# Hybrid attention/RG-LRU block with an MLP in three-pass split floats: order of casts, evacuations and low parts in the MLP, and the side of SBUF on which the output projection's pools lie

## The chip, the cores and the metric

The kernel runs on one core of a Trainium2 chip. The metric is the device time of one execution in microseconds (us). Three runs of the kernel before took 1237.33, 1234.93 and 1236.98 us (median 1236.98); a further, profiled execution took 1230.48 us. Engine names are those of the profile: PE (matmul), DVE (VectorE), ACT (ScalarE), POOL (GpSimd), SP (the engine on whose queue nearly all DMAs are issued).

## The reference

One transformer-like layer on 1024 tokens of width 1024: a normalised input goes to stick-breaking attention (8 heads) and a gated linear recurrence, their outputs together go through `w_out` and are added to `x`; then a squared-ReLU MLP (width 4096) is added.

```python
def reference(x, ...):
    h = rms_norm(x, norm1_g[l])
    x = x + hybrid_mixer(h, w_in[l], ..., w_out[l])     # concatenate([attn, lru], -1) @ w_out
    h = rms_norm(x, norm2_g[l])
    x = x + sq_relu_mlp(h, w_up[l], w_down[l])          # jnp.square(relu(h @ w_up)) @ w_down
    return x
```

## The kernel before

**Split floats.** Each operand of a large matmul is split in two parts: a *cast* on ACT rounds it to the PE's fast 32-bit format (the high part), and a subtraction on DVE or POOL makes the *low part* (value minus high part). A product is then three matmuls: low by high, high by low, high by high. In the MLP `split2` (cast on ACT, low part on DVE) makes both, `mmc` issues the three.

**Mixer.** Attention, the recurrence's gates and their projections run interleaved; their results go to `mix_d` in DRAM. Attention's score tiles, `vv`, `qT`, `kH`, `kL` of the odd head pairs and its work pool `ap` lie on the right side of SBUF; the weights of the projections (`wp`) and the even pairs' tiles (`qkvE`) lie on the left.

**Output projection.** For two halves of 512 output columns (n = 0, 1) and eight token tiles it multiplies `mix0`/`mix1` (high and low parts of `mix_d`, loaded through raw buffers `mr`) by `wo` (from `wr_o`). `raws` (raw buffers), `wf` (the split weights of n = 0) and `ra` lie on the right side, so on tiles that attention uses to its end; `mix`, `wn0` to `wn2` and `junk` lie on the left. Its results are added to `x1`, transposed into `h2` (PE, then ACT) and squared for the second norm (ACT into `junk`).

**MLP.** The products follow two groups of 16 of the 32 feature blocks, in a seven-product scheme with two levels. A group has 112 products of 12 matmuls (128x512): up products first (first sixteen, `a` and `b`, into tiles named `p1`; then triples with the movings `t2`, `b22`, `t3`; then pairs with `t1` and `t4`), then down products in four stages (`da`/`db`, `ea`/`eb`, `ga`/`gc`, `ha`). In a product one split operand is the *stationary* (`st`, `sb`, `sda`, ...) and one the *moving* (`m0t`, `m1t`, `mda`, ...). The list `PR` holds all 224 products; the loop at the end issues, for step q, the matmuls of product q (`pr.mm`), its bank evacuation (`pr.ev`), additional work hung on that step (`pr.after`: differences of `h2` and splits of new movings), a sum of `U` tiles eight products ahead (`usum`), the stationary of product q+6 (`stat`), the moving of product q+4 (`moving`), and loads of weights as raw buffers come free. From the fifth product on the scheduler keeps this written order on each engine (`keep_in_program_order`); before that it orders by its own simulation.

In the pairs `t1`/`t4` an evacuation is one or two DVE subtractions from the bank into `U`, followed on ACT by Relu and Square of those `U` tiles, and for one of three tiles by a POOL multiplication.

**Rings.** Stationaries rotate through six buffers, movings through twelve, raw weight blocks through eight (`Ring`: the first few of each in a pool that is open early, the rest in pools opened after the output projection). A tile that takes a buffer waits until the tile that had it twelve (six, eight) allocations earlier has been read. In the `ha` stage of the first group the casts of the second group's first movings (`m1b11`, `m1b21`) are hung on the steps, one on each, between the casts of `ha`'s own movings.

**Start of the MLP.** `mlp_head`, in the middle of the second half of the output projection, closes `wf` and `raws`, opens the first pools of the rings, loads the first two weight items (two blocks each) and splits the first movings and three stationaries.

Of the kernel before, what the change touches and what calls it, by code (L numbers as in the profile page):

```python
# [9 lines left out]
F32 = mybir.dt.float32  # L10
# [9 lines left out]
P = 128  # L20
S = 1024
D = 1024
# [21 lines left out]
def kernel(ctx, tc, x, norm1_g, w_in, conv_w, conv_b, w_rg, b_rg, w_ig, b_ig,  # L44
# [463 lines left out]
    wn1 = pool(tail, "wn1")  # L508
    junk = pool(tail, "junk").tile([P, D], F32, name="junk")
    wn2 = pool(tail, "wn2", bufs=2)  # L510
    mxp = pool(tail, "mix")
    mixes = [(mxp.tile([P, KC, 512], F32R, name=f"mix{g}h"), mxp.tile([P, KC, 512], F32R, name=f"mix{g}l")) for g in range(2)]
    wpools = {(0, u): wf for u in range(4)} | {(1, 0): wn0, (1, 2): wn1, (1, 3): wn2, (1, 1): wn2}

# [52 lines left out]

    rwr, stp, mvp = Ring(4, 4), Ring(3, 3), Ring(8, 4)
    rwr.pools[0] = raws
# [69 lines left out]
    def up_group(g):  # L639
        q0 = len(PR)  # L640

        def w(i, k, j):
            return w_up[k, 16 * g + 8 * i + j]
# [36 lines left out]

        its, bks = [], []
        for j in range(8):
            its.append(Item([(f"a{g}{j}", w(0, 0, j)), (f"b{g}{j}", w(0, 1, j))], lambda r: None))
            bks.append(banked(f"p1_{g}{j}"))
        ITEMS.extend(its)

        def pa_(j):
            prod(its[j], 0, "b11", bks[j], lambda: act.copy(U[:, j, 1], bks[j]()), True, False, 1)

        def pb_(j):  # L690
            prod(its[j], 1, "b21", bks[j], lambda: relu2(j, 0, bks[j]()), False, True, 1)

# [48 lines left out]
    def down_group(g):  # L741
# [17 lines left out]
        def prod(name, q, k, key, start, stop, item, r, free, ev=None, usum=None, store=None):  # L759
# [5 lines left out]
            def mv():  # L765
                pr.mv = split2(mvp, f"m{key}{g}{k}", item.raws[r])
                if store is not None:
                    act.dma_start(store, item.raws[r])

# [64 lines left out]
    def stat(n):  # L834
        nonlocal free
        if n < len(PR):
            pr = PR[n]
            pr.item.add()
            pr.stat()
            if pr.mov is None:  # L840
                free += pr.free
        load_items(n - NSTAT)

    def moving(n, q):
# [5 lines left out]
        load_items(q)  # L850

    def mlp_head():

        early.close()
        mvp.pools[0] = pool(ctx, "ma", bufs=8, side="right")
        stp.pools[0] = pool(ctx, "sa", bufs=3, side="right")
        load_items(-NSTAT)
        for u in range(4):
            mov("0b11", u, hb(0, 0, u))
        for n in range(3):  # L860
            stat(n)
        for u in range(4):
            mov("0b21", u, hb(1, 0, u))

# [6 lines left out]
    for n in range(2):  # L871
        wo = {}
        for grp in ((0, 1, 2), (3,), (4,), (5,), (6,), (7,)) if n == 0 else tuple((t,) for t in range(NT)):
# [3 lines left out]
            for u in KO:  # L877
                if u not in wo:
                    wr = raw(f"wr_o{n}{u}")
                    nc.sync.dma_start(wr, rows2(w_out, u, 512 * n))  # L880
                    wo[u] = split((nc.gpsimd, nc.vector)[(u + n) % 2], wpair(n, u), wr)
# [33 lines left out]

    for pl, nm, n in ((rwr, "rb", 4), (stp, "sb", 3), (mvp, "mb", 4)):
        pl.pools[1] = pool(ctx, nm, bufs=n)
    U = pool(ctx, "units").tile([P, 8, 4, 512], F32, name="U")
    nc.vector.tensor_scalar_mul(nrs2, rs2, -1.0)
    limit = len(ITEMS)  # L920
    load_items(-NSTAT)
    for n in range(3, NSTAT):
        stat(n)
    for q, pr in enumerate(PR):
        pinned = q >= PINNED
        pr.mm()
        pr.ev()
        for fn in pr.after:
            fn()
        if q + UAHEAD < len(PR) and PR[q + UAHEAD].usum is not None:  # L930
# [41 lines left out]
```

## Time and profile before

| | |
|---|---|
| three runs, median (lowest to highest) | 1236.98 us (1234.93 to 1237.33) |
| the profiled execution | 1230.48 us, of which 1228.7 us from first to last instruction |
| PE, DVE, ACT, POOL busy | 94%, 75%, 49%, 45% of the span |
| mixer up to its last attention matmul | to about 447 us |
| output projection, first to last matmul | 459.25 to 555.07 us |
| MLP | 555.07 to about 1225 us; the second group from 888.84 us |

Busy time of PE is that of pipelined matmuls, so it says little of the rate. The rate is read from the number of matmuls in a stretch of given length: a 128x512 matmul without a gap comes every 0.23 us at full clock. `L577` is the one line through which all MLP operations are recorded, so they are told apart by their tiles.

### The profile page before, as it was taken

The page shows a single profiled execution, that of the slowest core. Times are in us where ns is not written, and L with a number is a line of the kernel's source. Part 1 is how long each engine was busy: PE and PEld are TensorE (multiplying, and loading weights), DVE is VectorE, ACT ScalarE, POOL GpSimd, SP SyncE. Part 2 cuts the span into 40 slices and gives each one's busy share as a digit, 9 for nine tenths or more (in the row PEclk, how much of TensorE's full clock was granted, in tenths as well). Part 3 has the DMA queues.
Part 4 walks back from the last instruction along what each step waited for, and adds up shares of the span by engine and source line. Part 5 has one row for each costly group of instructions (what it writes and reads, how often), then busy time and mean ns, then how long its engine had stood idle before and what let it go on. Part 6 is the DMA issues. An engine that isn't in the chain of part 4 may idle for free.

```text
span 1228.7 us, 16111 instructions
## 1 busy us (share of the span) xinstructions
PE 1152.3 (94%) x5410; PEld 939.5 (76%) x5410; DVE 921.1 (75%) x1458; ACT 603.2 (49%) x1203; POOL 554.0 (45%) x506
## 2 busy tenths in 40 slices
PE   8998899899999949999999969999998999699998
PEld 7876787789887637888788848778886888487787
DVE  7889998999988845235767559997747665589975
ACT  7455466566566532156523554344445245544342
POOL 1366664654455733000342356853312524468632
PEclk9999899999999879999999989999999999799999
DMA  8210011401001636003333213445533332144465
GB/s 260 61 35 35 35 47 34 133 12 50 11 13 38 216 118 210 26 17 108 117 122 95 79 48 104 159 149 172 184 107 101 118 101 69 44 128 149 134 213 173
DMA packets 80787, 123.58 MB, mean 101 GB/s; under 512 B 10256, under 2 KB 28736, under 8 KB 80704
## 3 DMA queue, kind: packets, MB, share of 16 engines
q1 hardware_dynamic: 78400, 118.35, 31.5%
q10 hardware_dynamic: 2304, 4.20, 1.0%
q8 instruction: 43, 0.70, 0.3%
q14 instruction: 40, 0.33, 0.1%
HBM read 107.83 MB, written 14.68 MB: 100 GB/s over the span
## 4 chain that ended last, share of the span: by engine, by line
PE 60%; DVE 19%; issue 8%; ACT 7%; DMA 3%; POOL 2%; SPq 0%; DVEq 0%; ACTq 0%; POOLq 0%
PE p L577 18%; PE pa L577 11%; PE pb L577 4%; PE pc L577 4%; ACT U L577 3%; PE po L63 3%; PE po L64 2%; PE po L65 2%; DVE U L577 2%; PE pd L63 2%; PE pd L64 2%; PE pd L65 2%; DVE g L415 2%; PE av L435 2%; PE z L406 1%
## 5 line engine op out<-in xcount | busy, mean ns | idle before, releaser
L416 POOL TENSOR_TENSOR w<-w,g 128x128 f32<-128x128 f32 (+3 forms) x96 | 101.6, 1067 | 99.3 <-DVE g L415 44.3
L415 DVE TENSOR_TENSOR_SCAN g<-g 128x128 f32<-128x128 f32 (+3 forms) x96 | 111.6, 1173 | 5.3 <-ACT g L410 4.1
L577 POOL TENSOR_TENSOR U<-U 128x512 f32<-128x512 f32 x48 | 70.0, 1465 | 85.7 <-ACT U L577 69.4
L577 POOL TENSOR_TENSOR r_sb<-r_sb,r_sa 128x512 f32<-128x512 f32 x16 | 23.9, 1493 | 173.5 <-DMA r_sb<-in_w_up_dram 158.8
L63 PE MATMUL pd<-wh_p,hTl 128*128 128x384 f32 x256 | 91.7, 359 | 9.4 <-DVE vv L180 4.7
L577 PE MATMUL p<-m1t,st 128*128 128x512 f32 x384 | 91.6, 398 | 4.3 <-DVE U L577 4.3
L577 PE MATMUL p<-m0t,st 128*128 128x512 f32 x384 | 91.9, 398 | 2.3 <-DVE U L577 2.3
L64 PE MATMUL pd<-wl_p,hTh 128*128 128x384 f32 x256 | 90.7, 354 | 0.3 <-DVE wl_p L60 0.3
L577 DVE TENSOR_TENSOR U<-p,U 128x512 f32<-128x512 f32 x80 | 54.9, 686 | 47.0 <-PE p L577 47.0
L577 PEld LDWEIGHTS p<-m1t,st 128*128 128x128 f32 x384 | 73.1, 191 | 21.5 <-issue 4.7
L577 ACT ACTIVATE U<-U 128x512 f32<-128x512 f32 x96 | 58.9, 629 | 60.9 <-DVE U L577 59.5
L65 PE MATMUL pd<-wh_p,hTh 128*128 128x384 f32 x256 | 88.4, 345 | 0.0
L577 PEld LDWEIGHTS p<-m0t,st 128*128 128x128 f32 x384 | 73.1, 191 | 19.8 <-issue 2.7
L577 PE MATMUL p<-m1b,sb 128*128 128x512 f32 x288 | 68.1, 393 | 1.8 <-ACT U L577 1.8
L577 PE MATMUL p<-m0b,sb 128*128 128x512 f32 x288 | 68.7, 394 | 0.0
L577 PE MATMUL pa<-mda,sda 128*128 128x512 f32 x192 | 54.0, 434 | 15.6 <-ACT mda L577 12.6
L577 PEld LDWEIGHTS p<-m1b,sb 128*128 128x128 f32 x288 | 54.0, 188 | 14.5 <-ACT U L577 2.3
L577 PEld LDWEIGHTS p<-m0b,sb 128*128 128x128 f32 x288 | 53.8, 188 | 12.2
L410 ACT ACTIVATE g<-z 128x128 f32<-128x128 f32 (+3 forms) x96 | 48.1, 501 | 27.2 <-PE z L408 15.7
L577 PEld LDWEIGHTS pa<-mda,sda 128*128 128x128 f32 x192 | 40.3, 211 | 26.8 <-ACT mda L577 13.5
L63 PEld LDWEIGHTS pd<-wh_p,hTl 128*128 128x128 f32 x256 | 49.5, 194 | 13.5 <-DVE vv L180 6.2
L430 ACT CAST wth<-pw 128x512 fp32r<-128x512 f32 (+1 forms) x80 | 42.5, 548 | 34.4 <-PE pw L426 23.9
(302 smaller groups left out, 3229.9 us busy)
## 6 DMA issues: line engine op xcount, KB each, us to landing
wr_p<-in_w_in_dram SPq DMA_DIRECT2D x24, 192.0 KB, 2.6
xt<-in_x_dram SPq DMA_DIRECT2D x8, 512.0 KB, 6.8
x<-in_x_dram SPq DMA_DIRECT2D x16, 256.0 KB, 4.5
r_a<-in_w_up_dram SPq DMA_DIRECT2D x16, 256.0 KB, 2.8
r_b<-in_w_up_dram SPq DMA_DIRECT2D x16, 256.0 KB, 4.2
wr_o<-in_w_out_dram SPq DMA_DIRECT2D x8, 512.0 KB, 3.6
mr<-mix_d SPq DMA_DIRECT2D x8, 512.0 KB, 5.0
r_sa<-in_w_up_dram SPq DMA_DIRECT2D x16, 256.0 KB
```

The source lines that it names most:

```text
L63: nc.tensor.matmul(ps, al, bh, start=start, stop=False)
L64: nc.tensor.matmul(ps, ah, bl, start=False, stop=False)
L65: nc.tensor.matmul(ps, ah, bh, start=False, stop=stop)
L406: nc.tensor.matmul(z, qT[hs, h, qr], kL[hs, k0:k0 + kn], start=False, stop=not diag)
L410: nc.scalar.activation(g[:, :kn], z, AF.Sigmoid, scale=-1.0)
L415: nc.vector.tensor_tensor_scan(gr, gr, gr, g[:, kn:kn + 1], op0=ALU.mult, op1=ALU.bypass)
L416: nc.gpsimd.tensor_tensor(w[:, :kn], w[:, :kn], g[:, 1:kn + 1], op=ALU.mult)
L430: nc.scalar.copy(wth[:, :nw], pw[:, :nw])
L435: nc.tensor.matmul(av[:, q0:256], vv[:, 2 * m + jj, h, :], wt[:, 256 * jj:256 * jj + 256 - q0], start=m == 0 and jj == 0 and wt is wtl, st ...
L577: ins = getattr(self.eng, op)(*args, **kw)
```

## The change

Three things change.

1. In the MLP's loop the order within a step becomes: matmuls, casts of the stationary (q+6) and of the moving (q+4), evacuation, low parts of these casts, the work hung on the step, the low parts of that work, loads, `usum`. `split2` issues only the cast and puts the low part on a list that `low()` issues. The store of a summed weight block (`r2`) goes to that list too.
2. The second group's first movings are cast in the last four steps of `ha`, two on each, after all of `ha`'s own movings.
3. The output projection's raw buffers and first weights lie on the left, its `mix` tiles and other weights on the right; the raw buffers are four instead of three; the rings' early and late parts are 2+6 raw, 4+2 stationaries, 8+4 movings (before 4+4, 3+3, 8+4). The first up weights are loaded as items of one block instead of two, and the MLP's early loads are issued after the output projection's last weight load.

```diff
-    raws = pool(ctx, "ra", bufs=4, side="right")
+    raws = pool(ctx, "ra", bufs=2)
     early = ExitStack()
-    wf = pool(early, "wf", bufs=4, side="right")
-    rwp = pool(early, "raws", bufs=3, side="right")
+    rwp = pool(early, "raws", bufs=4)
+    wf = pool(early, "wf", bufs=4)
     tail = ExitStack()
-    wn0 = pool(tail, "wn0")
...
-    mxp = pool(tail, "mix")
+    mxp = pool(tail, "mix", side="right")
...
+    wn0 = pool(tail, "wn0", side="right")
...
-    rwr, stp, mvp = Ring(4, 4), Ring(3, 3), Ring(8, 4)
+    rwr, stp, mvp = Ring(2, 6), Ring(4, 2), Ring(8, 4)
...
+    lows = []
+
     def split2(pl, name, src):
+
         h, l = half(pl, name)
         act.copy(h, src)
-        dve.tensor_tensor(l, src, h.bitcast(F32), **sub)
+        lows.append(lambda: dve.tensor_tensor(l, src, h.bitcast(F32), **sub))
         return h, l
+
+    def low():
+        for fn in lows:
+            fn()
+        lows.clear()
...
+        for k in range(8):
             if g == 0:
-                after(q0 + k, lambda k=k: mov(f"1{('b11', 'b21')[k // 4]}", k % 4, hb(k // 4, 0, k % 4)))
+                after(q0 + 4 + k // 2, lambda k=k: mov(f"1{('b11', 'b21')[k // 4]}", k % 4, hb(k // 4, 0, k % 4)))
...
-    free, nload, limit = NRAW, 0, 2
+    free, nload, limit = 2, 0, 2
...
-        mvp.pools[0] = pool(ctx, "ma", bufs=8, side="right")
-        stp.pools[0] = pool(ctx, "sa", bufs=3, side="right")
-        load_items(-NSTAT)
...
+        stp.pools[0] = pool(ctx, "sa", bufs=4)
+        mvp.pools[0] = pool(ctx, "ma", bufs=8)
+        with tc.issue_after(last_w.ins):
+            load_items(-NSTAT)
...
-    limit = len(ITEMS)
+    limit, free = len(ITEMS), free + 6
...
     for q, pr in enumerate(PR):
         pinned = q >= PINNED
         pr.mm()
+        stat(q + NSTAT)
+        moving(q + MAHEAD)
         pr.ev()
+        low()
         for fn in pr.after:
             fn()
+        low()
+        load_items(q)
         if q + UAHEAD < len(PR) and PR[q + UAHEAD].usum is not None:
             PR[q + UAHEAD].usum()
-        stat(q + NSTAT)
-        moving(q + MAHEAD, q)
```

What this does to the order of instructions is shown at three places. First, ACT near the end of the first group's `t1`/`t4` pairs; `ACTIVATE U<-U` are the Relu and Square after an evacuation (three after a `t1` product, two after a `t4` product), `st10` and `st41` are casts of stationaries six products ahead, `sda00` and `sdb00` those of the first down products. Before:

```order
L577 CAST st41_7234<-r_tb05_7050 128x512
L577 ACTIVATE U_6199<-U_6199 128x512 x3
L577 CAST st10_7261<-r_ta06_7099 128x512
L577 ACTIVATE U_6199<-U_6199 128x512 x2
L577 CAST st41_7280<-r_tb06_7100 128x512
```

And now:

```order
L577 ACTIVATE U_6183<-U_6183 128x512 x2
L577 CAST st10_7255<-r_ta06_7099 128x512
L577 ACTIVATE U_6183<-U_6183 128x512 x3
L577 CAST st41_7277<-r_tb06_7100 128x512
L577 ACTIVATE U_6183<-U_6183 128x512 x2
```

The cast of `st10` for pair 6 stood behind the three activations of the same step and now stands ahead of them: each cast has moved up by one step's activations. On DVE the order of evacuations and low parts in these pairs is the same in both kernels.

Second, ACT at the end of the first group's `ha` stage; `mha` are casts of its movings, `m1b11x` and `m1b21x` (printed `m1b110` to `m1b213`) those of the second group's first movings, `sha` and `sb1` stationaries. Before:

```order
L577 CAST m1b110_8600<-h2_5412 128x512
L577 CAST sha06_8604<-U_6199 128x512
L577 CAST mha04_8607<-r_ha04_8507 128x512
L577 CAST m1b111_8626<-h2_5412 128x512
L577 CAST sha07_8630<-U_6199 128x512
L577 CAST mha05_8633<-r_ha05_8530 128x512
L577 CAST m1b112_8652<-h2_5412 128x512
```

And now:

```order
L577 CAST mha06_8648<-r_ha06_8557 128x512
L577 CAST sb110_8670<-r_a11_8609 128x512
L577 CAST mha07_8672<-r_ha07_8584 128x512
L577 CAST sb210_8694<-r_b10_8630 128x512
L577 CAST m1b110_8697<-h2_5412 128x512
L577 CAST m1b111_8699<-h2_5412 128x512
L577 CAST sb110_8717<-r_a12_8632 128x512
```

The first `m1b` cast stood ahead of `mha04`; now all of `mha` are cast before it. So of the twelve moving buffers the last eight allocations before the next movings (`m1t2`) are the eight `m1b`, and the four before these are `mha04` to `mha07`.

Third, ACT at the seam from attention to the output projection, a piece of the difference; `wth` and `ot` belong to the last attention blocks, `wo` are the output weights' high parts, `mix0h` that of the mixer's result.

```order
 L430 CAST wth3031_5168<-pw3031_5163 128x512
+L523 CAST wo01_5531<-wr_o01_5529 128x1024
 L430 CAST wth3032_5181<-pw3032_5176 128x512
 L430 CAST wth3033_5193<-pw3033_5189 128x384
 L440 COPY ot303_5201<-av303_5149 64x256
-L523 CAST wo00_5450<-wr_o00_5448 128x1024
-L887 CAST mix0h_5438<-mr00_5453 128x1024
-L523 CAST wo02_5477<-wr_o02_5475 128x1024
-L887 CAST mix0h_5438<-mr02_5480 128x1024
-L523 CAST wo03_5504<-wr_o03_5502 128x1024
```

The casts of the first half's four weights stood behind the last attention copy (`ot303`), one by one between the `mix0h` casts; now the last of the four (`wo01`) stands ahead of it and the other three still further up, between attention's activations. Their low parts have moved up likewise: `wo00` and `wo02` on POOL, `wo03` and `wo01` on DVE. On SP's queue the loads `wr_o00`, `mr00`, `wr_o02` and `mr02` stood behind the last attention store and the MLP's first four weight blocks, and now stand ahead of the sixteen loads of `x`:

```order
L443 DMA mix_d_87<-ob303_5202 64x256
L577 DMA r_a01_5945<-in_w_up_dram 128x512
L577 DMA r_b01_5946<-in_w_up_dram 128x512
L880 DMA wr_o00_5448<-in_w_out_dram 128x2x512
L885 DMA mr00_5453<-mix_d_87 128x2x512
```

And now:

```order
L889 DMA wr_o00_5448<-in_w_out_dram 128x2x512
L894 DMA mr00_5453<-mix_d_87 128x2x512
L443 DMA mix_d_87<-ob213_4675 64x256
L467 DMA mix_d_87<-hl30_5329 128x512
L889 DMA wr_o02_5475<-in_w_out_dram 128x2x512
L894 DMA mr02_5480<-mix_d_87 128x2x512
L906 DMA x1_5411<-in_x_dram 128x512 x2
```

The `mix0` casts themselves stay behind `ot303` on ACT, since `mix` now lies on attention's tiles.

More of the change, by code (lines that the diff above doesn't have):

```diff
@@ L678, in tt @@
             eng.tensor_tensor(o, a, b, **op)
[L681 to L685, printed above, removed]
+        bks = [banked(f"p1_{g}{j}") for j in range(8)]
         def pa_(j):
-            prod(its[j], 0, "b11", bks[j], lambda: act.copy(U[:, j, 1], bks[j]()), True, False, 1)
+            ITEMS.append(Item([(f"a{g}{j}", w(0, 0, j))], lambda r: None))
+            prod(ITEMS[-1], 0, "b11", bks[j], lambda: act.copy(U[:, j, 1], bks[j]()), True, False, 1)
         def pb_(j):
-            prod(its[j], 1, "b21", bks[j], lambda: relu2(j, 0, bks[j]()), False, True, 1)
+            ITEMS.append(Item([(f"b{g}{j}", w(0, 1, j))], lambda r: None))
+            prod(ITEMS[-1], 0, "b21", bks[j], lambda: relu2(j, 0, bks[j]()), False, True, 1)
         pa_(0)
@@ L767, in mv @@
                 if store is not None:
-                    act.dma_start(store, item.raws[r])
+                    lows.append(lambda: act.dma_start(store, item.raws[r]))
             def mm():
@@ L841, in stat, with moving @@
                 free += pr.free
-        load_items(n - NSTAT)
-    def moving(n, q):
+    def moving(n):
         nonlocal free
@@ L914 @@
     tail.close()
-    for pl, nm, n in ((rwr, "rb", 4), (stp, "sb", 3), (mvp, "mb", 4)):
-        pl.pools[1] = pool(ctx, nm, bufs=n)
-    U = pool(ctx, "units").tile([P, 8, 4, 512], F32, name="U")
+    U = pool(ctx, "units", side="right").tile([P, 8, 4, 512], F32, name="U")
+    for pl, nm, n in ((mvp, "mb", 4), (stp, "sb", 2), (rwr, "rb", 6)):
+        pl.pools[1] = pool(ctx, nm, bufs=n, side="right")
     nc.vector.tensor_scalar_mul(nrs2, rs2, -1.0)
-    limit = len(ITEMS)
+    limit, free = len(ITEMS), free + 6
     load_items(-NSTAT)
-    for n in range(3, NSTAT):
+    for n in range(2, NSTAT):
         stat(n)
+        low()
+        load_items(-NSTAT)
     for q, pr in enumerate(PR):
```

24 lines of the change are left out of this document (13 added, 11 removed).

## The prediction

> **What bounds the kernel now.** I read the page first, then the busy times in stretches of 25 us over the MLP. The page's rows (share of the span, then forty slices):
>
> ```profile
> PE 1152.3 (94%) x5410; PEld 939.5 (76%) x5410; DVE 921.1 (75%) x1458; ACT 603.2 (49%) x1203; POOL 554.0 (45%) x506
> PEclk9999899999999879999999989999999999799999
> ```
>
> PE is the only engine near its limit, and its clock dips in a few slices. Where it loses time shows in the stretches; the count behind PE's busy time is the number of matmuls.
>
> ```profile
> 600.00:625.00 25.00, 22.68 (x92) 17.99 (x91) 17.50 (x23) 8.50 (x15) 8.74 (x6) 0.93 0.39 118
> 650.00:675.00 25.00, 25.00 (x110) 20.27 (x109) 16.86 (x26) 10.07 (x17) 6.81 (x5) 1.00 0.33 95
> 700.00:725.00 25.00, 17.62 (x74) 13.61 (x72) 13.30 (x17) 13.38 (x24) 13.40 (x10) 0.90 0.15 43
> 725.00:750.00 25.00, 21.69 (x82) 17.17 (x83) 18.88 (x22) 13.94 (x25) 14.18 (x9) 0.89 0.30 85
> 750.00:775.00 25.00, 25.00 (x110) 20.32 (x109) 23.39 (x22) 10.28 (x18) 16.56 (x11) 1.00 0.43 126
> 925.00:950.00 25.00, 18.88 (x75) 14.68 (x74) 21.06 (x28) 15.80 (x30) 7.43 (x6) 0.93 0.36 106
> 1050.00:1075.00 25.00, 13.80 (x42) 10.03 (x41) 15.29 (x19) 14.37 (x26) 12.28 (x9) 0.73 0.12 33
> ```
>
> A stretch without a gap holds 110 matmuls, 25/110 = 0.227 us each, 2.73 us for a product of twelve. Missing matmuls count idle time and half-clock time together: 36 and 28 at 700 to 750 (14.5 us), 68 at 1050 (15.5 us), 18 at 600 (4.1 us), 35 at 925 (8.0 us). What the stalls wait for is read from the engines' timelines. First ACT, then DVE, near the end of the `t1`/`t4` pairs (start, us, tiles, idle time before and its releaser):
>
> ```profile
> 698.34 1.81 ACT L577 ACTIVATE U<-U 128x512 f32<-128x512 f32 x3 [1.36 <-DVE U L577]
> 700.06 0.60 ACT L577 CAST st<-r_ta 128x512 fp32r<-128x512 f32 x1
> 702.45 1.30 ACT L577 ACTIVATE U<-U 128x512 f32<-128x512 f32 x2 [1.79 <-DVE U L577]
> 703.65 0.60 ACT L577 CAST st<-r_tb 128x512 fp32r<-128x512 f32 x1
> ```
>
> ```profile
> 697.01 0.69 DVE L577 TENSOR_TENSOR st<-r_tb,st 128x512 fp32r<-128x512 f32 x1 [1.87 <-ACT st L577]
> 697.62 0.68 DVE L577 TENSOR_TENSOR U<-p,U 128x512 f32<-128x512 f32 x1
> 698.22 0.68 DVE L577 TENSOR_TENSOR U<-U,p 128x512 f32<-128x512 f32 x1
> 700.70 1.12 DVE L577 TENSOR_TENSOR st<-r_ta,st 128x512 fp32r<-128x512 f32 x1 [1.80 <-ACT st L577]
> 701.74 0.68 DVE L577 TENSOR_TENSOR U<-p,U 128x512 f32<-128x512 f32 x1
> 704.29 0.69 DVE L577 TENSOR_TENSOR st<-r_tb,st 128x512 fp32r<-128x512 f32 x1 [1.87 <-ACT st L577]
> ```
>
> This is a ring of waits in which PE has no part: DVE evacuates, ACT does Relu and Square of what it evacuated, only then casts, only then DVE can make the low part, and the next evacuation stands behind that. One turn for two products takes 704.29 - 697.01 = 7.28 us, and PE needs 2 x 2.73 = 5.46. Both engines are idle in between. The six products of lead run out, and PE stops:
>
> ```profile
> 723.07 0.79 PE L577 MATMUL pa<-mda,sda 128*128 128x512 f32 x1 [6.24 <-ACT mda L577]
> 735.52 0.96 PE L577 MATMUL pb<-mdb,sdb 128*128 128x512 f32 x3 [2.92 <-DVE U L577]
> ```
>
> **Casts ahead.** No operation is added or dropped; each cast on ACT moves ahead of one step's activations. Then a low part waits for a cast that waits for nothing of its own step but the matmuls, which free the stationary's buffer. Work per pair: ACT 1.81 + 0.60 + 1.30 + 0.60 = 4.31 us, DVE 0.69 + 0.68 + 0.68 + 1.12 + 0.68 = 3.85 us, both below 5.46, so PE sets the pace again. In the last two pairs the movings of the down products add two casts (1.2 us) and two low parts; with one of these at 1.78 (row below) DVE has 3.85 + 0.68 + 1.78 = 6.3 us, 0.85 over for two pairs, which six products of lead (16 us) cover. Should the cover be gone, it costs 1.7 us per group. The gain is at most 14.5 + 15.5 = 30.0 us, and nothing if the ring stays as it is; I take 28, since PE's rows in both groups show a full stop, and leave 1 us in each for what is late next. The down stages themselves have no activations on ACT, so nothing moves there but the stores of `r2` on ACT's queue, behind a low part: they are read a stage later. In the first up stage a copy from a bank now waits for one cast, 0.60 us; eight banks in rotation hide it.
>
> **Movings of the second group.** ACT, the two stops of PE that follow, and DVE just before the second:
>
> ```profile
> 925.62 0.62 ACT L577 CAST m1t<-U 128x512 fp32r<-128x512 f32 x1 [8.44 <-PE p L577]
> 929.49 5.73 PE L577 MATMUL p<-m1b,sb 128*128 128x512 f32 x24 [1.82 <-ACT U L577]
> 945.09 5.29 PE L577 MATMUL p<-m1t,st 128*128 128x512 f32 x15 [4.31 <-DVE U L577]
> 942.60 1.74 DVE L577 TENSOR_TENSOR st<-r_sb,st 128x512 fp32r<-128x512 f32 x1
> 944.26 0.68 DVE L577 TENSOR_TENSOR U<-p,U 128x512 f32<-128x512 f32 x1
> ```
>
> The cast of `m1t` stood 8.44 us for a moving buffer that PE still read: it was the buffer of an `m1b11` tile. With all of `mha` cast first, the buffer twelve allocations back is one of `mha`, long read. Everything behind it on ACT (stationaries, evacuations, eight more movings) is then on time, as in the first group, where allocations run that way already. So the loss becomes the first group's: 8.0 - 4.1 = 3.9 us. Moreover a low part of a stationary (0.68 us) no longer stands ahead of the evacuation on which PE waits there (in the last two rows it does): 0.6 in each group. I take 3.9 + 2 x 0.6 = 5.1 (bounds 0 and 8).
>
> **Seam to the output projection.** PE, SP, ACT, DVE and POOL:
>
> ```profile
> 446.67 0.27 PE L435 MATMUL av<-wth,vv 128*128 128x128 f32 x1
> 459.25 0.79 PE L63 MATMUL po<-wo,mix0l 128*128 128x512 f32 x1 [12.30 <-DVE mix0l L60]
> 449.48 0.43 SPq L880 DMA_DIRECT2D wr_o<-in_w_out_dram  x1
> 446.99 0.37 ACT L440 COPY ot<-av 64x256 f32<-64x256 f32 x1 [1.36 <-PE av L435]
> 456.26 1.04 ACT L887 CAST mix0h<-mr 128x1024 fp32r<-128x1024 f32 x1 [0.56 <-DMA mr<-mix_d]
> 463.23 1.23 DVE L60 TENSOR_TENSOR mix0l<-mr,mix0h 128x1024 fp32r<-128x1024 f32 x1 [4.04 <-ACT mix0h L887]
> 455.77 2.34 POOL L60 TENSOR_TENSOR wo<-wr_o,wo 128x1024 fp32r<-128x1024 f32 x1 [15.88 <-ACT wo L523]
> 420.76 1.70 POOL L465 TENSOR_TENSOR hl<-hl,gx 128x512 f32<-128x512 f32 x1 [3.17 <-DVE g L415]
> ```
>
> And the busy times of the stretch in which attention nears its end:
>
> ```profile
> 420.00:430.00 10.00, 10.00 (x29) 6.28 (x30) 8.88 (x12) 6.78 (x15) 9.24 (x8) 0.50 0.99 337
> ```
>
> The weights were loaded only when attention had freed its tiles, at 449.48, and PE stood 12.30 us. Now weights and two `mr` blocks come during attention; after the last attention matmul remain the copy `ot`, one `mix0h` cast and one `mix0l`: 0.32 + 0.37 + 1.04 + 1.23 and some 0.2 between, 3.1 us. That is 9.2 us less. But the four weight splits now run inside attention's last 35 us, where POOL and DVE are busy (9.24 and 8.88 of 10 us in the last row): POOL 2 x 2.34 = 4.7, of which its idle 3.17 ahead of 420.76 can take most, 1.5 left; DVE 2 x 1.23 = 2.5, one of them between the last serial steps; the ACT casts in its gaps. I put attention's end 1.5 + 1.23 + 0.8 = 3.5 us later, the last term for DVE instructions slowed beside POOL's (bounds 0 and 4.7 + 2.5 = 7.2), and the gain at 9.2 - 3.5 = 5.7 (bounds 2 and 9.2; -2 if a `mr` block behind the `x` loads came 4 us late). On SP, `wr_o03` waits for POOL's low part of `wo00` with attention's stores behind it; the first reader of these stores (`mr11`) is the last of the mixer's blocks to be loaded.
>
> The remaining gap at the seam will be some 3 us. In this trace a gap of 2.3 us (two matmuls between 608 and 610) was already followed by half clock, and the projection's start, after 12.30 us, ran at it too; PE's busy time, matmuls and granted clock:
>
> ```profile
> 608.00:610.00 2.00, 0.45 (x2) 1.00 0.06 21
> 612.00:614.00 2.00, 2.00 (x6) 0.50 0.62 160
> 459.00:462.00 3.00, 2.75 (x7) 0.50 0.74 241
> ```
>
> So I keep the slow start of the projection as it is, at no gain. The Trainium skill ("TensorE: Matmul & The Clock Gate", section "Why this matters for your kernels") asks only for no idle gap above about 3 us between bursts; by that the projection could start at full clock, 12 matmuls instead of 7 in its first 2.75 us, 1.1 us better. But the rows show half clock after a gap below 3 us, and the measurement decides.
>
> **Start of the MLP.** Only two stationaries are ready instead of three, and six raw buffers open late; one of them overlies `junk`, read until the last norm. PE has two products, 5.5 us, and transposes to do meanwhile. I take 0.5 us of loss (bounds 0 and 3).
>
> **Sum.** -28 - 5.1 - 5.7 + 0.5 = -38.3: the profiled execution of 1230.48 us (span 1228.7, 1.8 around it) would be 1192.2. The runs shown have their median at 1236.98, 6.5 above it; on that basis 1198.7, say **1199**.
>
> **Rivals.** *Attention pays for the seam.* The splits cost all they save: the seam gains 0, time 1199 + 5.7 = 1205. For it: POOL is full at 420 to 430. Against: its 3.17 us hole just before.
>
> *DVE becomes the bound behind the ring.* POOL's two-input operations slow DVE's low parts:
>
> ```profile
> 796.59 1.78 DVE L577 TENSOR_TENSOR mea<-r_ea,mea 128x512 fp32r<-128x512 f32 x1
> ```
>
> If every low part in the last pairs and in `da`/`db` takes 1.78 instead of 0.68, four of them need 7.1 us per pair against 5.46, 1.65 x 8 = 13 us per group, of which the lead hides half: 2 x 7 = 14 us of the 28 are lost, time 1213. Against: from 750 to 775 PE has its 110 matmuls while DVE is busy 23.39. The Trainium skill speaks for this rival ("SBUF — State Buffer", section "Who interferes with whom"): VectorE with two SBUF inputs and GpSimd hold one port pair in turn, each for its whole instruction. The 1.78 against 0.68 agrees.
>
> *The ring does not open*, because casts and evacuations both wait for the same matmuls: only 5.1 + 5.7 - 0.5 remain, 1227.
>
> *Slower: the first up stages become load-bound.* Only two raw buffers are open until the tail closes, items are loaded one by one at the end of a step, and a late raw block now holds ACT's evacuation behind its cast. The page's landing time of such blocks:
>
> ```profile
> r_b<-in_w_up_dram SPq DMA_DIRECT2D x16, 256.0 KB, 4.2
> ```
>
> If each of the 32 `a`/`b` products of both groups waits out 4.2 instead of 2.73 us, that costs 47 us: 1199 + 47 = 1246. It decides from 2.73 + 38/32 = 3.9 us per product on. Against: eight blocks are in rotation, some 20 us ahead.
>
> **How the numbers follow.** Forecast 0.62, seam paid for 0.16, DVE bound 0.12, ring closed 0.04, load-bound 0.04; 0.02 for ends that meet. The range takes the forecast's bounds (-30 - 8 - 9.2 gives 1190) up to the DVE rival, 1213: 1190 to 1213. Within 0.2% (2.5 us, about what a measurement of this kernel can tell from no change) only the last 0.02: faster 0.94, same 0.02, slower 0.04.
>
> **What would show it.** Stretches in both `t1`/`t4` to `da` passages with about 110 matmuls per 25 us; ACT without waits for `U` of 1.8 us before each Relu; no ACT wait for PE near `m1t`; at the seam `wo` casts among attention's and a PE gap near 3 us. Wrong it would be if PE again waits for `mda`, if DVE is full with PE short of 110 in `da`/`db`, or if `p` products wait for `sb` and its load.

## The result and the profile after

| | before | after |
|---|---|---|
| median of the first comparison (4 runs each) | 1236.33 us (1234.93 to 1237.33) | 1188.9 us (1187.34 to 1192.23) |
| ratio, 95% interval | | 0.9621 (0.9596 to 0.9645) |
| profiled execution, its span | 1230.48, 1228.7 | 1190.02, 1188.2 |
| second comparison, beside other kernels | 1233.01 (13 runs) | 1188.73 (4 runs), ratio 0.9633 (0.9596 to 0.967) |

The change saves 44 to 47 us. The prediction was 1199 with a range of 1190 to 1213: the direction was right, and so was the mechanism in the main; the time came out 10 us below the forecast and 1 us outside the range.

The page's rows of the kernel after (share of the span; granted clock in forty slices):

```profile
PE 1140.8 (96%) x5410; PEld 936.0 (79%) x5410; DVE 934.5 (79%) x1458; ACT 603.7 (51%) x1203; POOL 541.1 (46%) x506
PEclk9998999999999978999999999999999999999999
```

No slice inside the MLP is below 9 any more (the stretch from 900 to 925 us below still shows a granted 0.93); a dip is left in the mixer, in the fourth slice, and one around the seam to the output projection. Busy times in stretches of 25 us (the number behind PE's time counts its matmuls):

```profile
600.00:625.00 25.00, 23.71 (x104) 19.13 (x104) 20.40 (x27) 8.70 (x15) 12.02 (x8) 1.00 0.35 116
700.00:725.00 25.00, 25.00 (x111) 20.46 (x110) 22.47 (x25) 17.37 (x31) 16.32 (x11) 1.00 0.21 64
725.00:750.00 25.00, 25.00 (x110) 20.36 (x109) 20.07 (x19) 10.27 (x18) 15.41 (x10) 1.00 0.37 107
800.00:825.00 25.00, 22.91 (x101) 18.55 (x100) 21.67 (x30) 9.13 (x16) 7.04 (x6) 1.00 0.53 163
900.00:925.00 25.00, 22.38 (x92) 18.02 (x91) 20.71 (x26) 14.87 (x27) 7.21 (x5) 0.93 0.26 86
1025.00:1050.00 25.00, 25.00 (x111) 20.53 (x110) 23.43 (x22) 13.13 (x23) 16.48 (x11) 1.00 0.30 86
1100.00:1125.00 25.00, 23.62 (x101) 18.54 (x100) 25.00 (x32) 10.90 (x20) 11.22 (x7) 1.00 0.53 168
```

Both passages from `t1`/`t4` to `da`/`db` (700 to 750 and, 30 us earlier than before, around 1025) run without a gap. What is left are mainly stretches of 92 to 104 matmuls, where PE waits between 1.3 and 2.6 us, twice near the start of the second up stage (600, 900) and twice at the start of `ga`/`gc` (800, 1100):

```profile
607.00 5.76 PE L577 MATMUL p<-m0t,st 128*128 128x512 f32 x24 [1.29 <-DVE U L577]
805.94 3.00 PE L577 MATMUL pc<-mgc,sgc 128*128 128x512 f32 x12 [2.09 <-ACT sga L577]
921.68 7.21 PE L577 MATMUL p<-m1t,st 128*128 128x512 f32 x24 [2.62 <-DVE U L577]
1121.05 2.98 PE L577 MATMUL pc<-mgc,sgc 128*128 128x512 f32 x12 [1.38 <-ACT sga L577]
```

DVE's timeline in `t1`/`t4` answers to the ring of before:

```profile
692.60 0.69 DVE L577 TENSOR_TENSOR U<-p,U 128x512 f32<-128x512 f32 x1 [1.35 <-PE p L577]
693.21 0.68 DVE L577 TENSOR_TENSOR U<-U,p 128x512 f32<-128x512 f32 x1
693.81 0.68 DVE L577 TENSOR_TENSOR st<-r_ta,st 128x512 fp32r<-128x512 f32 x1
695.35 0.69 DVE L577 TENSOR_TENSOR U<-p,U 128x512 f32<-128x512 f32 x1 [0.86 <-PE p L577]
696.00 0.81 DVE L577 TENSOR_TENSOR st<-r_tb,st 128x512 fp32r<-128x512 f32 x1
698.14 0.69 DVE L577 TENSOR_TENSOR U<-p,U 128x512 f32<-128x512 f32 x1 [1.33 <-PE p L577]
```

A turn for two products now takes 698.14 - 692.60 = 5.54 us, where it took 7.28, and every evacuation waits for PE's bank, none for ACT: PE sets the pace. The low part follows without a wait.

The seam shows another picture. The last gate product, the last attention matmul and the first of the projection:

```profile
416.00 0.39 PE L65 MATMUL pgl<-hTh,wh_gl 128*128 128x512 f32 x1
456.02 0.28 PE L435 MATMUL av<-wth,vv 128*128 128x128 f32 x1
458.97 0.79 PE L63 MATMUL po<-wo,mix0l 128*128 128x512 f32 x1 [2.67 <-DVE mix0l L60]
554.10 2.01 PE L577 MATMUL p<-m0b,sb 128*128 128x512 f32 x8
```

The gap shrank from 12.30 to 2.67 us, but attention ends at 456.30 instead of 446.94. Of these 9.4 us, 2.9 had been lost before the last gate product, in work that this change does not touch. They are put down to chance: before's own second profile (below) is 2.0 us later there than its first, and the second profile of the kernel after is 2.6 us earlier than its first. So the seam is measured from the end of the last gate product on.

### The profile page after: what moved, and what is told of

Same layout as the page of the kernel before. It is cut to its first block, busy times and chain, and to the rows that moved or that the text cites. A ratio compares the mean times of both kernels' runs of the same rounds, so it can differ in the third digit from the quotient of the medians.

```text
span 1188.2 us, 16104 instructions
## 1 busy us (share of the span) xinstructions
PE 1140.8 (96%) x5410; PEld 936.0 (79%) x5410; DVE 934.5 (79%) x1458; ACT 603.7 (51%) x1203; POOL 541.1 (46%) x506
## 4 chain that ended last, share of the span: by engine, by line
PE 70%; DVE 16%; issue 5%; DMA 3%; ACT 3%; POOL 2%; SPq 0%; DVEq 0%; ACTq 0%; POOLq 0%
PE p L577 24%; PE pa L577 11%; PE pb L577 5%; PE pc L577 4%; PE po L63 3%; PE po L64 3%; PE po L65 3%; DVE g L415 2%; PE av L435 2%; PE pd L63 2%; PE pd L64 2%; PE pd L65 2%; PE z L406 2%; PE pw L426 2%; POOL r_ea L577 1%
## 5 line engine op out<-in xcount | busy, mean ns | idle before, releaser
L430 ACT CAST wth<-pw 128x512 fp32r<-128x512 f32 (+1 forms) x80 | 42.6, 547 | 37.5 <-PE pw L426 25.5
L60 DVE TENSOR_TENSOR wtl<-pw,wth 128x512 fp32r<-128x512 f32 (+1 forms) x80 | 49.3, 628 | 9.9 <-ACT wth L430 9.5
L426 PE MATMUL pw<-ident,w 128*128 128x128 f32 x288 | 48.2, 285 | 5.4 <-DVE wtl L60 3.0
```

The source lines that it names most:

```text
L60: eng.tensor_tensor(lo, src, hi.bitcast(F32), op=ALU.subtract)
L426: nc.tensor.transpose(pw[:, i * P:(i + 1) * P], wrow[rr][j // 4][:, j % 4 * P:(j % 4 + 1) * P], ident)
L430: nc.scalar.copy(wth[:, :nw], pw[:, :nw])
```

## The experiments

Times of parts come from PE's timelines: attention from the end of the last gate product to the end of the last `av`; "to projection" from the same point to the first `po`; MLP from the first `p` to the end of the last `pa`. Ratios are to runs of the kernel before on the same chip; times of parts are of one profile each. With the old seam, attention takes 33.4 to 36.0 us from profile to profile.

| kernel | median us | ratio, 95% | attention | to projection | MLP |
|---|---|---|---|---|---|
| before, two profiles | 1234.67 | 1.0013 (0.9994-1.0032) | 33.5, 35.5 | 45.8, 48.5 | 669.7, 670.3 |
| order alone | 1197.26 | 0.9716 (0.9684-0.9747) | 34.5 | 47.1 | 636.1 |
| casts ahead, low parts too | 1246.67 | 1.0110 (1.0068-1.0152) | 33.8 | 46.0 | 682.2 |
| moved casts alone | 1229.7 | 0.9980 (0.9960-0.9999) | 36.0 | 48.2 | 666.0 |
| order and moved casts | 1194.5 | 0.9699 (0.9671-0.9726) | 33.4 | 45.7 | 632.4 |
| seam alone | 1227.23 | 0.9955 (0.9934-0.9976) | 38.2 | 40.9 | 671.2 |
| after, two profiles | 1188.73 | 0.9633 (0.9596-0.9670) | 39.9, 40.1 | 42.6, 42.7 | 630.3, 630.6 |
| after, late splits | 1192.05 | 0.9656 (0.9610-0.9701) | 38.5 | 44.6 | 630.8 |
| after, splits behind `mix0h` | 1187.56 | 0.9625 (0.9595-0.9654) | 37.6 | 40.2 | 630.4 |
| after, sums first | 1187.74 | 0.9632 (0.9599-0.9664) | 39.9 | 42.6 | 630.9 |
| three changes together | 1182.69 | 0.9583 (0.9554-0.9613) | 37.6 | 40.3 | 627.2 |
| the same, split on DVE | 1180.76 | 0.9567 (0.9538-0.9596) | 36.5 | 39.2 | 628.9 |

### The kernel before again

> The kernel before, unchanged, profiled a second time. The profiled execution on which the prediction's sum was made took 1230.5 us, its other runs 1234.9 to 1237.3: 6 us lie in a place that the first profile did not show. Theory A (front part and attention vary from execution to execution): this profile shows the MLP at 670 us again (333.6 + 336) and the extra time before 555 us. Theory B (the two passages from t1/t4 to da/db vary): the MLP takes up to 676 us and the stops of PE there are longer than 14.5 + 15.5 us. Ratio 1.000 in either.

Its last gate product, the last `av`, the first `po` and the first `p`:

```profile
415.13 0.39 PE L65 MATMUL pgl<-hTh,wh_gl 128*128 128x512 f32 x1
450.79 0.27 PE L435 MATMUL av<-wth,vv 128*128 128x128 f32 x1
463.98 0.79 PE L63 MATMUL po<-wo,mix0l 128*128 128x512 f32 x1 [12.92 <-DVE mix0l L60]
559.72 1.99 PE L577 MATMUL p<-m0b,sb 128*128 128x512 f32 x8
```

Theory A holds: the MLP takes 670.3 us as in the first profile (669.7), and the projection starts 463.98 - 459.25 = 4.7 us later; 2.0 of these come before the last gate product, 2.1 in attention, 0.6 in the gap. PE's stops in the passages are the same to a tenth of a us. The kernel before varies from 1227.5 to 1239.95 us over all its runs, with medians of 1233.0 to 1236.3 in the comparisons.

### Casts ahead, with the low parts last or first

```diff
         pr.mm()
+        stat(q + NSTAT)
+        moving(q + MAHEAD)
         pr.ev()
+        low()
         for fn in pr.after:
             fn()
+        low()
+        load_items(q)
...
-        stat(q + NSTAT)
-        moving(q + MAHEAD, q)
```

> The kernel before with the order of a step alone changed: casts ahead of the evacuation, low parts behind the evacuation; pools, seam and the mha/m1b casts as before. Theory (the ring between ACT and DVE opens): the two passages lose their 30.0 us, PE at 110 matmuls per 25 us there, and the low part before the evacuation goes: 28 to 31 us less, ratio 0.975 to 0.977. Rival (the seam and the later casts carry a good part of the 47 us): under 22 us, ratio above 0.982. Rival (ordinary runs lose more in the passages than the profiled one did): 36 us, ratio 0.971.

The order alone is worth 33.9 us in the MLP (the mean of before's two profiles, 670.0, less 636.1) and a ratio of 0.9716: more than the 0.975 to 0.977 of the theory, and the size of the second rival. That rival's cause is out, since before's second profile shows the passages and the MLP as the first; where the surplus lies is told below. The second kernel differs only in a `low()` ahead of `pr.ev()`, so that each low part moves ahead together with its cast:

> The kernel before with casts ahead of the evacuation and the low parts also ahead of it. If the ring is what was slow, this does not open it: evacuation, activations, the next step's cast, its low part, the next evacuation still follow one another within one step, so a turn takes the 7.3 us as before and PE stops for mda and U again: ratio 0.99 to 1.005. Rival (it is the cast's place on ACT alone that counts, the low part's place on DVE only a fraction of a us): ratio 0.972 to 0.978, as with the full order.

It is 13 us slower than before, and slower than the 1.005 expected at most. DVE's timeline of this kernel in `t1`/`t4`:

```profile
694.88 1.12 DVE L577 TENSOR_TENSOR st<-r_tb,st 128x512 fp32r<-128x512 f32 x1 [1.80 <-ACT st L577]
695.93 0.68 DVE L577 TENSOR_TENSOR U<-p,U 128x512 f32<-128x512 f32 x1
698.48 0.69 DVE L577 TENSOR_TENSOR st<-r_ta,st 128x512 fp32r<-128x512 f32 x1 [1.87 <-ACT st L577]
699.08 0.69 DVE L577 TENSOR_TENSOR U<-p,U 128x512 f32<-128x512 f32 x1
699.69 0.68 DVE L577 TENSOR_TENSOR U<-U,p 128x512 f32<-128x512 f32 x1
702.16 1.12 DVE L577 TENSOR_TENSOR st<-r_tb,st 128x512 fp32r<-128x512 f32 x1 [1.80 <-ACT st L577]
```

A turn takes 702.16 - 694.88 = 7.28 us, to the hundredth the turn of before, although every cast stands ahead of its step's activations. The cast still stands behind the activations of the step before, its low part behind it, and the evacuation behind the low part: the same ring, with the same waits of 1.80 and 1.87 us. In the kernel with the order alone, DVE's order of evacuations and low parts in these pairs is the one of before; the cast has moved ahead of one step's activations and its low part has stayed behind the evacuation, so the chain from evacuation to cast to low part reaches the evacuation two steps on. So a cast that takes its low part along opens nothing; it opens where the low part stays. The loss against before lies in `da`/`db` (60.5 and 59.6 us in the two groups, before 52.2 and 53.5), where the movings' low parts too stand ahead of the evacuation (PE's timeline):

```profile
720.85 5.26 PE L577 MATMUL pa<-mda,sda 128*128 128x512 f32 x12 [4.43 <-ACT mda L577]
732.42 1.65 PE L577 MATMUL pb<-mdb,sdb 128*128 128x512 f32 x3 [3.39 <-DVE U L577]
737.60 1.64 PE L577 MATMUL pb<-mdb,sdb 128*128 128x512 f32 x3 [3.54 <-DVE U L577]
```

### Moved casts, and the kernel after without its seam

```diff
+        for k in range(8):
             if g == 0:
-                after(q0 + k, lambda k=k: mov(f"1{('b11', 'b21')[k // 4]}", k % 4, hb(k // 4, 0, k % 4)))
+                after(q0 + 4 + k // 2, lambda k=k: mov(f"1{('b11', 'b21')[k // 4]}", k % 4, hb(k // 4, 0, k % 4)))
```

> The kernel before with the casts of the second group's movings alone moved, from one in each of the eight ha steps to two in each of the last four. Theory: the ACT wait of 8.44 us for a buffer at m1t goes, and the second group's early stops fall from 8.0 to about 4.1 us: 3.9 us less, ratio 0.997. Rival (ACT's wait was idle time that hid behind other waits): under 1 us, ratio 0.999 to 1.000.

The MLP is 670.0 - 666.0 = 4.0 us shorter, as the theory has it. The interval of the ratio (0.9960 to 0.9999) holds the expected 0.997, but also the rival's 0.999; the profile decides. ACT's wait of 8.44 us is gone, PE's stop of 1.82 us with it, and the stop of 4.31 us at `m1t` has become 2.23, the first group's 2.3. (The second group alone is 5.6 us shorter than in before's first profile; 1.9 us of that are lost again in the first group's `da`/`db`, which the edit does not touch.)

> The kernel after without its seam: order of a step and the moved casts as in the changed kernel, pools and output projection as in the kernel before. Theory (as predicted): 28 + 5.1 us less than before, ratio 0.973, so that the seam is worth some 5 us. Rival (attention pays for the seam): as fast as the changed kernel within 1.5 us but for the start of the MLP, ratio 0.962 to 0.964. By the two profiles the seam is worth 0.3 us as it ran and about 3 us if the later start of the front part (2.9 us) is chance.

The MLP takes 632.4 us, again 3.7 less than with the order alone (636.1): the two parts add up. The ratio is 0.9699, where 0.973 was expected. Against 0.9633 and 0.9621 it leaves the seam 8 to 10 us, with intervals that overlap; the parts give it less: 4.6 us up to the first product of the MLP, 4.2 of them up to the projection's start (46.9, the mean of the six profiles with the old seam, less 42.7), and 2 us in the MLP.

### The seam alone, and who pays for it

> The kernel after with the step's order and the mha/m1b casts put back: what is left is the seam (pools on the other side, the rings that follow from them, single items for a and b). Theory (seam gains some 3 to 5 us at the projection's start, rings 0 to 2 us): ratio 0.994 to 0.998. Rival (attention pays in full): 0.998 to 1.000. Rival (the seam carries the rest of the 47 us): 0.992.

Pools, rings and single items alone, with the old order of a step, gain 5.5 us. To the projection's start it takes 40.9 us instead of 46.9: the gap is 9.8 shorter (2.67 against 12.4) and attention 3.8 longer (38.2 against 34.4; the old values are the means of the six profiles with the old seam).

In the kernel after attention pays more, 40.0 - 34.4 = 5.6 us. Its DVE timeline shows with what; first one row of the kernel before:

```profile
417.41 0.69 DVE L463 SCALAR_TENSOR_TENSOR ge<-ge,gx 128x512 f32<-128x512 f32 x1
```

Then the kernel after, DVE and ACT:

```profile
420.74 2.47 DVE L463 SCALAR_TENSOR_TENSOR ge<-ge,gx 128x512 f32<-128x512 f32 x1
440.81 1.45 DVE L60 TENSOR_TENSOR wo<-wr_o,wo 128x1024 fp32r<-128x1024 f32 x1 [0.64 <-ACT wo L523]
453.28 1.22 DVE L60 TENSOR_TENSOR wo<-wr_o,wo 128x1024 fp32r<-128x1024 f32 x1
```

```profile
418.57 1.05 ACT L523 CAST wo<-wr_o 128x1024 fp32r<-128x1024 f32 x1 [2.16 <-DMA wr_o<-in_w_out_dram]
439.74 1.05 ACT L523 CAST wo<-wr_o 128x1024 fp32r<-128x1024 f32 x1
452.20 1.05 ACT L523 CAST wo<-wr_o 128x1024 fp32r<-128x1024 f32 x1
```

The gate operation `ge` runs beside POOL's first split and takes 2.47 us instead of 0.69. The two splits of DVE, the last two rows of each fence, stand with cast and low part among the serial steps, ahead of a scan `g` and of a `wtl` for which PE waits. PE's two longest stops in this stretch:

```profile
423.73 0.58 PE L435 MATMUL av<-wtl,vv 128*128 128x256 f32 x1 [2.30 <-DVE ob L441]
445.24 0.58 PE L435 MATMUL av<-wtl,vv 128*128 128x256 f32 x1 [5.00 <-DVE wtl L60]
```

Two variants hold three of the four splits back, the first behind attention's last copy `ot`, the second behind the first `mix0h` cast (the second's edit):

```diff
-                    wo[u] = split(...)
+                    with tc.issue_after(first.ins) if n == 0 and u != KO[0] else nullcontext():
+                        wo[u] = split(...)
```

> The kernel after with three of the four splits of the first half's output weights (two of DVE, one of POOL) held behind attention's last copy; the first split stays in attention. If these splits are what attention pays with, its end comes 3 to 5 us earlier, counted from the last gate product, the gap ahead of the projection stays near 2.7 us, and the time is 3 to 5 us below the kernel after: ratio to before 0.958 to 0.960. Rival (the DMA queues with the early loads are what delays attention, or the projection now waits for the late splits): within 1 us of the kernel after or slower, 0.962 to 0.965.

> As the kernel with three splits of output weights held back, but held behind the first cast of the mixer's block instead of the last attention copy, so that they no longer stand ahead of it. Expected, if the splits in attention cost some 1.5 us and the longer gap came only from their place in the queues: attention from the last gate product to its end 38.5 us (40.0 in the kernel after), gap 2.7 us, MLP unchanged at 630.5 us: 1.5 us below the kernel after. Rival (later splits make PE wait at the second block of the projection): gap 2.7 us, but a new wait inside the projection, no gain.

Behind `ot`, attention is 1.5 us shorter, not the 3 to 5 expected, and the gap grows to 6.06 us, because two casts of weights and one low part (2.54 us) now stand ahead of the mixer's block on ACT and DVE. Behind `mix0h` the gap stays at 2.67, attention is 2.4 us shorter than in the kernel after, and PE finds its second block in time; the timed runs (ratio 0.9625 against 0.9633) cannot tell this from no change. Three of the four splits thus cost attention about 2.4 of the 5.6 us; with them held back, the stop of 5.00 us is still one of 3.40.

### The new stops, and three changes together

> The kernel after with the sums of units for the product eight steps on issued at the start of a step instead of its end. Theory: the new stop at the start of the ga/gc stage (PE for ACT's cast of sga, 2.1 and 1.4 us) comes from the sum on DVE that stands behind the low parts and the evacuation of four banks (2.7 us); then it goes, 2 to 4 us less in the MLP (627 to 628 us against 630.5). Rival (the evacuations alone delay PE, for the banks): no change of the MLP.

The theory fell. The stop at `ga`/`gc` is gone, but stops of 0.3 to 0.9 us have come in around the starts of `ea`/`eb` and `ga`/`gc` instead, and the MLP takes 630.9 us. It seems that DVE's evacuation of four banks costs there whichever of its instructions is in front; this was not tried further.

> Both of these and, third, two of the four casts of the m0t/m1t movings for t3 moved one step later, since four of their low parts (3.6 us) stand ahead of the evacuation for which PE waits 2.6 us at m1t. Expected: 1.5 + 3 + 2 us below the kernel after, ratio to before 0.958 to 0.960. Rival (what is late is only passed on): 0.962 to 0.964.

The third change moves two casts of a moving by a step, so that two instead of four low parts stand ahead of the evacuation at the second up stage:

```diff
-            after(q0 + 15, lambda u=u: mov(f"{g}t3", u, U[:, 4 + u, 2]))
+            after(q0 - 1 + u // 2, lambda u=u: mov(f"{g}t3", u, U[:, 4 + u, 2]))
```

(`q0` is that of the next stage in the new line.) The MLP is down to 627.2 us and the time to 1182.69, ratio 0.9583: 6 us below the kernel after, with an interval that overlaps that one's a little. As the sums gave nothing by themselves and the splits act ahead of the MLP, the 3.3 us in the MLP are put down to this third change, though it was not run alone; they lie where it acts (second and third up stages 111.0 and 111.9 us, with the sums alone 111.7 and 114.8; PE's stop at `m1t` 1.42 us, with the sums alone 2.79).

> As the kernel with the three changes together (1182.7 us), but the low parts of the first half's output weights change engines: those of blocks 0 and 2 on DVE, those of 3 and 1 on POOL. So the one split that stays in attention no longer runs on POOL (2.34 us) beside DVE's gate operation (2.01 us there, 0.69 without POOL beside it in the kernel before). Theory (POOL's two-input operation is what slows the gate): the gate operation takes 0.69 us again, DVE gains 1.3 and gives 1.2 for its own low part, PE's stop of 1.83 us at the next av shrinks by about 1 us, and attention ends 0 to 1 us earlier: ratio 0.957 to 0.959. Rival (DVE is the tighter engine of the two): attention ends 1 us or more later.

The same gate operation on DVE in this last kernel, ahead of it the split that was POOL's:

```profile
417.08 1.50 DVE L60 TENSOR_TENSOR wo<-wr_o,wo 128x1024 fp32r<-128x1024 f32 x1 [0.41 <-ACT wo L523]
418.50 0.68 DVE L60 TENSOR_TENSOR wtl<-pw,wth 128x512 fp32r<-128x512 f32 x1
419.11 0.68 DVE L463 SCALAR_TENSOR_TENSOR ge<-ge,gx 128x512 f32<-128x512 f32 x1
```

With POOL idle the gate operation takes 0.68 us, and attention is 1.1 us shorter than with the split on POOL. Of its 5.6 us, 2.4 and 1.1 are thus accounted for; the other 2.1 stay open, and are no more than the profiles with the old seam differ by. The Trainium skill ("SBUF — State Buffer", section "Who interferes with whom") lets a DVE instruction with two SBUF inputs wait for GpSimd's port; the 2.47 and 2.01 us beside POOL against 0.68 without it agree. With 1180.76 us (ratio 0.9567) this is the fastest kernel of the study, 8 us below the kernel after; from the kernel with the split on POOL (0.9583) the ratios' intervals do not tell it apart. In its profile the projection is 1.6 us shorter (92.8 us against 94.4) and the MLP 1.7 us longer, and neither was expected; the first is the clock's doing (last section).

## Why the prediction was right in kind and too small in size

Two steps failed: the term of the casts and low parts in the sum (-29.2 us, measured -33.9) was too small, and the basis of 1236.98 us to which the sum was added was 1 to 4 us above the medians that the kernel before has in later comparisons. The terms beside what was measured in the parts (profiles; the sum of the four is -44.2 us, and the comparisons show 44 to 47):

| step | predicted | measured |
|---|---|---|
| casts ahead, and low parts off the evacuation (-28 - 1.2) | -29.2 | -33.9 |
| moved `m1b` casts | -3.9 | -3.7 to -4.0 |
| seam, to the first product of the MLP | -5.7 | -4.6 |
| rings and pools in the MLP | +0.5 | -2.0 |

- **Casts ahead: right, and the term that was mis-sized most.** The stages of the MLP in us, first and second group (from the first product of one stage to that of the next in PE's timeline):

| | first up | second and third up | `da`/`db` | `ea`/`eb` | `ga`/`gc` | `ha` |
|---|---|---|---|---|---|---|
| before | 46.4, 46.4 | 121.6, 123.3 | 52.2, 53.5 | 47.0, 46.7 | 44.2, 44.2 | 22.2, 22.1 |
| order alone | 46.4, 46.4 | 112.4, 113.5 | 44.3, 44.1 | 44.7, 45.6 | 45.7, 48.6 | 22.2, 22.1 |
| order and moved casts | 46.4, 44.2 | 112.4, 112.0 | 44.3, 44.1 | 44.7, 45.6 | 45.7, 48.6 | 22.1, 22.1 |
| after | 45.9, 43.8 | 111.7, 114.5 | 44.1, 43.8 | 45.0, 45.1 | 46.5, 45.5 | 22.1, 22.1 |

  From the start of the second up stage to the end of `da`/`db`, both groups together, before takes 350.6 us and the order alone 314.3: 36.3 less, against 29.2 in the sum. The prediction counted 30.0 us of missing matmuls in three stretches of the passages and took 2 off for "what is late next". Nothing was late next there (110 and 111 matmuls in each stretch, above). At the second up stages it gave the low part 0.6 us a group. There the stretches of 25 us miss 6 matmuls with the order alone instead of 18 in the first group, 22 instead of 35 in the second: 2.7 and 3.0 us. PE's stop itself shrank from 2.32 to 1.15 and from 4.31 to 2.65 us, and the granted clock of these stretches is 1.00 instead of 0.93. The term held the low part's time and nothing for the clock behind the stop, which falls in some profiles and not in others (last section), so part of this surplus is luck. In the later stages, where the prediction moved nothing, `ea`/`eb` gained 3.4 us and `ga`/`gc` lost 5.9 (the new wait for `sga`). That the low part must not move ahead with its cast the prediction did not say; the run with low parts first shows it.
- **Movings of the second group: right**, in mechanism and size, alone and on top of the order (there the stop at `m1t` falls to 1.14 us, like the first group's).
- **Seam: the sum nearly right, two terms not.** The gap closed by 9.8 us, not 9.2, but attention paid 5.6, not 3.5. The bound of 7.2 held. The rival "attention pays for the seam" describes half of what happened. Beyond POOL's and DVE's own time, which the prediction added up, PE's stop of 5.0 us inside attention brings half clock (last section).
- **Start of the MLP: wrong in sign.** The first up stages are 0.5 and 0.4 us shorter than with the old seam, and `ga`/`gc` of the second group takes 45.5 instead of 48.6. No stop of PE there is for a load. That the new rings are what gains is argued, not shown: with the old order of a step they gain nothing (671.2 against 670.0).
- **The rivals:** DVE is busy 25.00 of 25 us around 1100 with 101 matmuls, but the passages are full: DVE does not bind behind the ring. It seems to bind later, at `ea`/`eb` and `ga`/`gc`, where the prediction did not look; which of its instructions is in the way there is open. The ring opened, and no product of the first up stages waited for its load.
- **The distance to the range.** Of the 10 us between forecast and result, 5.9 are the sum (-38.3 against -44.2). The other 4 are put down to the basis: the three runs of before with their median at 1236.98 were at the upper end of what that kernel does, 1233 to 1236 in the later comparisons. On that basis even the measured parts give 1192.8, inside the range; it took both errors to leave it. That it is the basis is argued, not shown: in the first comparison before had 1236.33, so 3 us of its saving lie in no part that the profiles show, and why that kernel varies by 1% was not followed beyond the front part and attention. The lower end of 1190 also took "at most 30.0 us" for a bound of the casts' gain, though it was a count over the stretches that showed a loss, not over all that the order touches.

## What to carry to other kernels

When two engines wait for each other in turn, write down the ring as a list of instructions, step by step, and count how many steps it spans. Here it opened when the cast moved ahead of a step's activations while its low part stayed behind the evacuation; with the low part moved along, the turn stayed at 7.28 us and the kernel lost 13 us. Work moved under a busy stretch is not free: put it behind the first instruction that the next stage needs, not merely behind the last of the stage before (a gap of 2.67 us against 6.06), and look at what runs beside it (the gate operation took 2.01 us beside POOL's split, 0.68 without). A bound counted from the stretches that show a loss is no bound for a change that touches all of them, and three runs are a narrow basis for a kernel that varies by 1%.

## What the hardware showed

The granted clock falls inside attention towards the end of a stop of 5.0 us and stays at half for some 5 us of work (1.7 + 2.0 + 1.4; a mean between 1.00 and 0.50, the levels at which the rows stay, is read as time at one and the other). Stretches of 2 us of the kernel after, around that stop and around the gap (PE's matmuls, then granted clock as third number from the end):

```profile
440.97:442.97 2.00, 0.00 (x0) 0.00 (x0) 2.00 (x2) 1.76 (x4) 2.00 (x2) 1.00 0.15 33
444.97:446.97 2.00, 1.73 (x9) 1.73 (x9) 1.96 (x4) 0.00 (x0) 0.76 (x1) 0.50 0.43 160
446.97:448.97 2.00, 2.00 (x10) 1.69 (x9) 0.89 (x2) 0.71 (x2) 1.09 (x1) 0.50 0.00 0
448.97:450.97 2.00, 2.00 (x13) 2.00 (x14) 0.56 (x1) 0.61 (x2) 0.00 (x0) 0.64 0.00 0
...
456.97:458.97 2.00, 0.00 (x1) 0.01 (x1) 1.47 (x3) 2.00 (x3) 0.00 (x0) 0.57 0.45 148
458.97:460.97 2.00, 2.00 (x5) 1.61 (x6) 1.07 (x1) 1.52 (x2) 1.29 (x1) 0.50 0.43 93
...
462.97:464.97 2.00, 2.00 (x8) 1.64 (x7) 1.96 (x1) 0.00 (x0) 1.72 (x1) 0.72 0.85 293
```

By an estimate from these rows, the stop's second price is about 2.6 us of PE's time, half of the work at half clock. At the seam the same gap of 2.67 us had different consequences. In the kernel after the clock is down when the projection starts; in the kernel with the splits behind `mix0h` it falls only during the first matmuls:

```profile
454.01:456.01 2.00, 0.00 (x0) 0.00 (x1) 1.42 (x2) 2.00 (x3) 0.29 (x1) 1.00 0.15 33
456.01:458.01 2.00, 2.00 (x6) 1.61 (x7) 1.38 (x1) 1.53 (x2) 2.00 (x1) 0.68 0.41 78
458.01:460.01 2.00, 2.00 (x6) 1.52 (x6) 2.00 (x2) 0.21 (x1) 0.19 (x1) 0.50 0.48 184
```

In the fastest kernel, behind a gap of 2.66 us, it does not fall at all:

```profile
452.71:454.71 2.00, 2.00 (x9) 1.66 (x10) 2.00 (x2) 1.53 (x2) 0.39 (x1) 1.00 0.45 84
454.71:456.71 2.00, 2.00 (x10) 1.64 (x9) 0.21 (x1) 0.24 (x1) 2.00 (x1) 1.00 0.98 309
```

The work at half clock is 5.1 us in the first case (2.0 + 2.0 + 0.56 x 2.0, as a mean of 0.72 is 0.56 of the time at half), some 3.4 in the second (0.64 x 2.0, 2.0 and little more) and none in the third, and the projection takes 95.1, 94.4 and 92.8 us: roughly half of the work at half clock is lost. The MLP shows the same in one kernel: the kernel after stops for 2.62 us at `m1t` in its first profile and for 2.60 in its second, and the stretch from 900 to 925 us holds 92 matmuls at a granted 0.93 in the first and 99 at 1.00 in the second. So the prediction's reading, no full-clock start behind a gap of some 3 us, held for the kernel after but is no rule: whether and when the clock falls behind such a gap is not settled by the gap's length alone. The Trainium skill ("TensorE: Matmul & The Clock Gate", section "Part 1: The HAM clock gate") has the clock follow an activity window that runs free of the kernel, so that the point of change shifts with its phase; these cases agree.
